# A FiLM layer on one core: other queues for the loads, whole-slab stores, a narrower matmul, program order

## The chip, the cores and the metric

The kernel runs on one core of a Trainium2 chip. The metric is the device time of one execution in microseconds (us). A core has TensorE (PE, matrix products), VectorE (DVE), ScalarE (ACT), GpSimd (POOL) and SyncE (SP). Data move between the main memory and the on-chip memory by 16 DMA engines; in this kernel SP and ACT issue the transfers, and each of the two has a queue of its own on these engines.

## The reference

```python
batch, seq, dim = 32, 512, 256
cond_dim = 64

def reference(x, conditioning, gamma_proj, beta_proj):
    gamma = conditioning @ gamma_proj
    beta = conditioning @ beta_proj
    return (x * (1 + gamma[:, None, :]) + beta[:, None, :]).astype(np.float32)
```

All arrays are float32. x and the output have 32 x 512 x 256 elements, 16.8 MB each. The two projections are small: 32x64 by 64x256.

## The kernel before

The rows of x (batch and seq together, 256 elements each) are cut into four slabs of eight batch entries, 4 MB each. In a slab, partition p holds 32 successive rows, 32 KB, that lie one after the other in the main memory. All four slabs have their own tile (`xs`), so no load ever waits for a buffer. Sixteen partitions belong to one batch entry.

The loads: ACT issues the three small ones, conditioning (`cond_s`, 8 KB), gamma_proj and beta_proj (the two halves of `gbproj`, 64 KB each; lines 48 to 51). SP issues x (line 59): slab 0 in two parts of 8 and 24 rows per partition, the other slabs whole.

The scales: each partition needs the gamma and beta row of its batch entry. An identity of 32x32 is made on GpSimd and each of its columns repeated 16 times on VectorE (`rident`, line 67). One matmul of the conditioning against it gives the transposed conditioning with each column repeated, 64x512 (line 72); VectorE copies it out of PSUM (line 74). For each slab a matmul with 128 of these columns and `gbproj` gives gamma and beta for all 128 partitions, 128x512 in PSUM (`gb_p`, line 79). ACT copies them to `gb_s`, adding one to gamma (lines 82 and 85), because GpSimd works from there; VectorE reads PSUM itself.

The main loop goes over the slabs, and in each over two groups of 16 rows. VectorE takes the first 11 rows of a group and GpSimd the other 5. Each does a multiplication and an addition in place: lines 100 and 103 on VectorE, 102 and 104 on GpSimd. Then ACT issues the store of the group: 16 rows of 128 partitions, 2 MB, in runs of 16 KB (line 105).

A scheduler of the language sets the order of each engine's instructions and places the waits. On VectorE it keeps the order of the program. On GpSimd it puts both multiplications of a slab ahead of both additions. DMA completions are counted on eight semaphores that are used in turn, so the ninth DMA of the program and later ones can wait for the DMA that used the same one before: the last load of x waits in this way for gamma's load.

Of the kernel before, what the change touches and what calls it, by code (L numbers as in the profile page):

```python
# [2 lines left out]

# [5 lines left out]


@with_exitstack
def kernel(
    ctx: ExitStack,
    tc: tile.TileContext,
    x: bass.AP,
    conditioning: bass.AP,
    gamma_proj: bass.AP,
    beta_proj: bass.AP,
    out: bass.AP,  # L20
):
    nc = tc.nc
    f32 = mybir.dt.float32
    ALU = mybir.AluOpType

    batch, seq, dim = x.shape
    cond_dim = conditioning.shape[1]
    P = 128
    SLABS = 4
    BS = batch // SLABS  # L30
    REP = P // BS
    ROWS = BS * seq // P
    assert SLABS * BS == batch and REP * BS == P and ROWS * REP == seq

    x_v = x.flatten_outer_dims().rearrange("(s p r) d -> s p r d", s=SLABS, p=P)
    o_v = out.flatten_outer_dims().rearrange("(s p r) d -> s p r d", s=SLABS, p=P)

    LOADS = {0: [8, 24]}
    GROUP = 16
    ON_DVE = 11  # L40

    consts = ctx.enter_context(tc.tile_pool(name="consts", bufs=1))
    xpool = ctx.enter_context(tc.tile_pool(name="xpool", bufs=1))
    psum = ctx.enter_context(tc.tile_pool(name="psum", bufs=1, space=bass.MemoryType.PSUM))


    cond_s = consts.tile([batch, cond_dim], f32)
    nc.scalar.dma_start(out=cond_s, in_=conditioning)  # L48
    gbproj = consts.tile([cond_dim, 2 * dim], f32)
    nc.scalar.dma_start(out=gbproj[:, :dim], in_=gamma_proj)  # L50
    nc.scalar.dma_start(out=gbproj[:, dim:], in_=beta_proj)

    slabs = []
    for s in range(SLABS):
        xs = xpool.tile([P, ROWS, dim], f32, name=f"xs{s}")
        slabs.append(xs)
        r = 0
        for n in LOADS.get(s, [ROWS]):
            nc.sync.dma_start(out=xs[:, r : r + n, :], in_=x_v[s, :, r : r + n, :])
            r += n  # L60
        assert r == ROWS


    ident = consts.tile([batch, batch], f32)
    make_identity(nc, ident)
    rident = consts.tile([batch, batch * REP], f32)
    nc.vector.tensor_copy(  # L67
        out=rident.rearrange("p (b g) -> p b g", g=REP),
        in_=ident.to_broadcast([batch, batch, REP]),
    )  # L70
    cond_T_p = psum.tile([cond_dim, batch * REP], f32)
    nc.tensor.matmul(cond_T_p, lhsT=cond_s, rhs=rident, start=True, stop=True)  # L72
    cond_T = consts.tile([cond_dim, batch * REP], f32)
    nc.vector.tensor_copy(out=cond_T, in_=cond_T_p)  # L74

    gb_p, gb_s = [], []
    for s in range(SLABS):
        p_t = psum.tile([P, 2 * dim], f32, name=f"gb_p{s}")
        nc.tensor.matmul(p_t, lhsT=cond_T[:, s * P : (s + 1) * P], rhs=gbproj,  # L79
                         start=True, stop=True)  # L80
        s_t = consts.tile([P, 2 * dim], f32, name=f"gb_s{s}")
        nc.scalar.activation(out=s_t[:, :dim], in_=p_t[:, :dim],  # L82
                             func=mybir.ActivationFunctionType.Identity,
                             bias=1.0, scale=1.0)
        nc.scalar.copy(out=s_t[:, dim:], in_=p_t[:, dim:])  # L85
        gb_p.append(p_t)
        gb_s.append(s_t)

    def rows(t, n):
        return bass.AP(tensor=t.tensor, offset=t.offset, ap=[t.ap[0], [0, n], t.ap[1]])  # L90

    for s in range(SLABS):
        xs = slabs[s]
        g_p, b_p = gb_p[s][:, :dim], gb_p[s][:, dim:]
        g_s, b_s = gb_s[s][:, :dim], gb_s[s][:, dim:]
        for r0 in range(0, ROWS, GROUP):
            v = xs[:, r0 : r0 + ON_DVE, :]
            w = xs[:, r0 + ON_DVE : r0 + GROUP, :]
            nv, nw = ON_DVE, GROUP - ON_DVE
            nc.vector.scalar_tensor_tensor(out=v, in0=rows(g_p, nv), scalar=1.0, in1=v,  # L100
                                           op0=ALU.add, op1=ALU.mult)
            nc.gpsimd.tensor_tensor(out=w, in0=w, in1=rows(g_s, nw), op=ALU.mult)  # L102
            nc.vector.tensor_add(out=v, in0=v, in1=rows(b_p, nv))  # L103
            nc.gpsimd.tensor_tensor(out=w, in0=w, in1=rows(b_s, nw), op=ALU.add)  # L104
            nc.scalar.dma_start(out=o_v[s, :, r0 : r0 + GROUP, :],
                                in_=xs[:, r0 : r0 + GROUP, :])


# [1 line left out]
_INS = ['x', 'conditioning', 'gamma_proj', 'beta_proj']  # L110
_OUTS = [((32, 512, 256), 'float32')]


# [23 lines left out]
```

## Time and profile before

| what | value |
|---|---|
| three runs | 84.4, 85.82, 86.3 us; median 85.82 |
| profiled execution | 84.35 us |
| its span, first to last instruction | 82.6 us |
| VectorE busy | 49.9 us (60%) |
| GpSimd busy | 46.2 us (56%) |
| TensorE busy | 9.1 us (11%) |
| DMA | 33.69 MB, mean 408 GB/s over the span |
| first operation on x | 17.3 us (GpSimd), 17.5 us (VectorE) |
| first and last store issued | 25.9 and 66.7 us |
| stores, issue to landing | 15.1 to 22.6 us |

The page gives the busy time of each engine, then rows of 40 digits, each digit the busy tenths of a slice of 2.06 us, then the DMA queues (q1 is SP's, q10 is ACT's), the chain of work that ended last, the groups of instructions with their mean duration, and the DMA issues with their time from issue to landing. The same tables can be asked for a stretch of the span only.

### The profile page before, as it was taken

What the parts mean: (1) busy time and instruction counts of PE and PEld (TensorE: products, weight loads), DVE (VectorE), ACT (ScalarE), POOL (GpSimd) and SP (SyncE); (2) the same over time, 40 slices, a digit from 0 to 9 for tenths busy, and PEclk for the clock granted to TensorE, in tenths of its full rate; (3) what the DMA queues carried; (4) which work ended last, traced back from release to release, by engine and by line L of the source; (5) the groups of instructions that cost most, each with busy time, mean ns of one, the idle gap of its engine ahead of it and who ended that gap; (6) DMA issues with size and microseconds to landing.
All of it is one profiled execution on the core that took longest, in us unless ns stands there. A gap on an engine that the chain in (4) does not pass through costs nothing.

```text
span 82.6 us, 156 instructions
## 1 busy us (share of the span) xinstructions
PE 9.1 (11%) x10; PEld 2.8 (3%) x10; DVE 49.9 (60%) x18; ACT 3.9 (5%) x9; POOL 46.2 (56%) x22
## 2 busy tenths in 40 slices
PE   0080000899600000000000000000000000000000
PEld 0100000443000000000000000000000000000000
DVE  2011000059999999999999999999999920000000
ACT  0600000034400000000000000000000000000000
POOL 2000000069999999999999999999995000000000
DMA  3899999969969989998889979899999999999992
GB/s 56 337 508 397 389 397 524 460 302 508 508 270 492 508 381 381 413 476 381 381 381 556 460 302 460 381 468 421 429 452 389 468 421 421 460 389 452 437 421 87
DMA packets 2080, 33.69 MB, mean 408 GB/s; under 512 B 288, under 2 KB 416, under 8 KB 416
## 3 DMA queue, kind: packets, MB, share of 16 engines
q1 hardware_dynamic: 720, 16.78, 48.6%
q10 hardware_dynamic: 1360, 16.92, 48.0%
HBM read 16.92 MB, written 16.78 MB: 408 GB/s over the span
## 4 chain that ended last, share of the span: by engine, by line
DVE 49%; DMA 16%; issue 11%; PE 2%; ACTq 1%; ACT 1%
DVE xs L100 30%; DVE xs L103 19%; DMA gbproj<-in_beta_proj_dram 16%; PE gb_p L79 2%; ACTq L50 1%; ACTq L48 0%; ACT gb_s L82 0%; ACT gb_s L85 0%
## 5 line engine op out<-in xcount | busy, mean ns | idle before, releaser
L102 POOL TENSOR_TENSOR xs<-xs,gb_s 128x1280 f32<-128x1280 f32 x8 | 23.0, 2895 | 16.2 <-ACT gb_s L82 16.2
L100 DVE SCALAR_TENSOR_TENSOR xs<-gb_p,xs 128x2816 f32<-128x2816 f32 x8 | 24.7, 3083 | 10.9 <-ACT gb_s L85 10.9
L103 DVE TENSOR_TENSOR xs<-xs,gb_p 128x2816 f32<-128x2816 f32 x8 | 24.7, 3086 | 0.3
L104 POOL TENSOR_TENSOR xs<-xs,gb_s 128x1280 f32<-128x1280 f32 x8 | 23.0, 2893 | 0.0
L79 PE MATMUL gb_p<-gbproj,cond_T 64*128 64x512 f32 x8 | 7.2, 1074 | 8.9 <-DMA gbproj<-in_beta_proj_dram 8.9
L74 DVE COPY cond_T<-cond_T_p 64x512 f32<-64x512 f32 x1 | 0.7, 683 | 4.3 <-PE cond_T_p L72 4.3
L79 PEld LDWEIGHTS gb_p<-gbproj,cond_T 64*128 64x128 f32 x8 | 2.5, 328 | 13.7 <-issue 13.7
L72 PE MATMUL cond_T_p<-rident,cond_s 32*64 32x512 f32 x2 | 1.9, 1065 | 3.9 <-DMA cond_s<-in_conditioning_dram 3.9
L82 ACT ACTIVATE gb_s<-gb_p 128x256 f32<-128x256 f32 x4 | 1.5, 383 | 16.4 <-PE gb_p L79 16.4
L85 ACT COPY gb_s<-gb_p 128x256 f32<-128x256 f32 x4 | 1.5, 367 | 0.0
L82 ACT ACT_TABLE_LOAD x1 | 1.3, 1283 | 2.4 <-issue 2.4
L67 DVE COPY rident<-ident 32x512 f32<-32x512 f32 x1 | 0.4, 416 | 1.2 <-POOL ident masks.py:199 1.2
L72 PEld LDWEIGHTS cond_T_p<-rident,cond_s 32*64 32x64 f32 x2 | 0.3, 202 | 3.9 <-issue 3.9
masks.py:197 POOL MEMSET ident<- 32x32 f32 x1 | 0.1, 114 | 0.3 <-POOLq L121 0.3
masks.py:199 POOL TENSOR_SCALAR_AFFINE_SELECT ident<-ident 32x32 f32<-32x32 f32 x1 | 0.2, 202 | 0.1
L121 POOL MEMSET const-float32-0.0<- 128x1 f32 x1 | 0.1, 103 | 0.2 <-issue 0.2
L121 POOL MEMSET const-bfloat16-1.0<- 128x1 bf16 x1 | 0.1, 106 | 0.0
L121 POOL MEMSET const-uint8-127<- 128x1 uint8 x1 | 0.1, 106 | 0.0
L121 POOL MEMSET const-float32-1.0<- 128x1 f32 x1 | 0.1, 103 | 0.0
## 6 DMA issues: line engine op xcount, KB each, us to landing
out_dram<-xs ACTq DMA_DIRECT2D x8, 2048.0 KB, 18.2
xs<-in_x_dram SPq DMA_DIRECT2D x3, 4096.0 KB, 32.9
xs<-in_x_dram SPq DMA_DIRECT2D x1, 3072.0 KB, 12.2
xs<-in_x_dram SPq DMA_DIRECT2D x1, 1024.0 KB, 4.6
gbproj<-in_gamma_proj_dram ACTq DMA_DIRECT2D x1, 64.0 KB, 9.1
gbproj<-in_beta_proj_dram ACTq DMA_DIRECT2D x1, 64.0 KB, 12.9
cond_s<-in_conditioning_dram ACTq DMA_DIRECT2D x1, 8.0 KB, 3.0
```

Source lines behind the costliest of these rows:

```text
L50: nc.scalar.dma_start(out=gbproj[:, :dim], in_=gamma_proj)
L67: nc.vector.tensor_copy(out=rident.rearrange("p (b g) -> p b g", g=REP), in_=ident.to_broadcast([batch, batch, REP]),)
L72: nc.tensor.matmul(cond_T_p, lhsT=cond_s, rhs=rident, start=True, stop=True)
L74: nc.vector.tensor_copy(out=cond_T, in_=cond_T_p)
L79: nc.tensor.matmul(p_t, lhsT=cond_T[:, s * P : (s + 1) * P], rhs=gbproj, start=True, stop=True)
L82: nc.scalar.activation(out=s_t[:, :dim], in_=p_t[:, :dim], func=mybir.ActivationFunctionType.Identity, bias=1.0, scale=1.0)
L85: nc.scalar.copy(out=s_t[:, dim:], in_=p_t[:, dim:])
L100: nc.vector.scalar_tensor_tensor(out=v, in0=rows(g_p, nv), scalar=1.0, in1=v, op0=ALU.add, op1=ALU.mult)
L102: nc.gpsimd.tensor_tensor(out=w, in0=w, in1=rows(g_s, nw), op=ALU.mult)
L103: nc.vector.tensor_add(out=v, in0=v, in1=rows(b_p, nv))
L104: nc.gpsimd.tensor_tensor(out=w, in0=w, in1=rows(b_s, nw), op=ALU.add)
L121: nc = _bacc.Bacc("TRN2", target_bir_lowering=False, num_devices=1)
```

## The change

It has four parts. The first 8 rows per partition of x are loaded by ACT; the three small loads go to SP, ahead of the rest of x. The matmul that transposes the conditioning uses the plain 32x32 identity and gives 64x32; the 16-fold repetition is made afterwards, for each slab, in VectorE's copy out of PSUM (four copies of 64x128 for one of 64x512). Each slab is stored at once, 4 MB in runs of 32 KB, after both of its groups of 16 rows. The main loop stands in a block that keeps the order of the program, so that GpSimd multiplies and adds one group before it takes the next. The sizes of slabs and groups, and the 11 to 5 split of rows, are as before. The last load of x now waits for the first load of x instead of gamma's.

```diff
-    LOADS = {0: [8, 24]}
-    GROUP = 16
-    ON_DVE = 11
+    SLABS = [(8, [8, 24]), (8, [32]), (8, [32]), (8, [32])]
+    STORES = [[32], [32], [32], [32]]
+    PIECE, ON_DVE = 16, 11
...
+    def load(eng, s, i):
+        sl = slabs[s]
+        r = sum(sl["loads"][:i])
+        n = sl["loads"][i]
+        eng.dma_start(out=sl["xs"][:, r : r + n, :], in_=sl["src"][:, r : r + n, :])
...
-    nc.scalar.dma_start(out=cond_s, in_=conditioning)
-    nc.scalar.dma_start(out=gbproj[:, :dim], in_=gamma_proj)
-    nc.scalar.dma_start(out=gbproj[:, dim:], in_=beta_proj)
...
-        for n in LOADS.get(s, [ROWS]):
-            nc.sync.dma_start(out=xs[:, r : r + n, :], in_=x_v[s, :, r : r + n, :])
...
+    load(nc.scalar, 0, 0)
+    nc.sync.dma_start(out=cond_s, in_=conditioning)
+    nc.sync.dma_start(out=gbproj[:, :dim], in_=gamma_proj)
+    nc.sync.dma_start(out=gbproj[:, dim:], in_=beta_proj)
+    load(nc.sync, 0, 1)
+    load(nc.sync, 1, 0)
+    load(nc.sync, 2, 0)
+    load(nc.sync, 3, 0)
...
-    rident = consts.tile([batch, batch * REP], f32)
-    nc.vector.tensor_copy(
-        out=rident.rearrange("p (b g) -> p b g", g=REP),
-        in_=ident.to_broadcast([batch, batch, REP]),
-    )
-    cond_T_p = psum.tile([cond_dim, batch * REP], f32)
-    nc.tensor.matmul(cond_T_p, lhsT=cond_s, rhs=rident, start=True, stop=True)
-    cond_T = consts.tile([cond_dim, batch * REP], f32)
-    nc.vector.tensor_copy(out=cond_T, in_=cond_T_p)
...
+    cond_T_p = psum.tile([cond_dim, batch], f32)
+    nc.tensor.matmul(cond_T_p, lhsT=cond_s, rhs=ident, start=True, stop=True)
+    for s, sl in enumerate(slabs):
...
+        c_t = consts.tile([cond_dim, P], f32, name=f"cond_T{s}")
+        nc.vector.tensor_copy(
+            out=c_t.rearrange("p (b g) -> p b g", g=rep),
+            in_=cond_T_p[:, b0 : b0 + n].to_broadcast([cond_dim, n, rep]),
+        )
...
+        nc.tensor.matmul(p_t, lhsT=c_t, rhs=gbproj, start=True, stop=True)
...
-            nc.scalar.dma_start(out=o_v[s, :, r0 : r0 + GROUP, :],
-                                in_=xs[:, r0 : r0 + GROUP, :])
+    with tc.manual_schedule():
+        for s, sl in enumerate(slabs):
...
+            for n in STORES[s]:
+                for q0 in range(done, done + n, PIECE):
...
+                nc.scalar.dma_start(out=sl["dst"][:, done : done + n, :],
+                                    in_=xs[:, done : done + n, :])
```

More of the change, by code (lines that the diff above doesn't have):

```diff
@@ L28 @@
     P = 128
[L29 to L36, printed above, removed]
-    LOADS = {0: [8, 24]}
-    GROUP = 16
-    ON_DVE = 11
+    SLABS = [(8, [8, 24]), (8, [32]), (8, [32]), (8, [32])]
+    assert sum(n for n, _ in SLABS) == batch
+    STORES = [[32], [32], [32], [32]]
+    PIECE, ON_DVE = 16, 11
+    x_f = x.flatten_outer_dims()
+    o_f = out.flatten_outer_dims()
     consts = ctx.enter_context(tc.tile_pool(name="consts", bufs=1))
@@ L44 @@
     psum = ctx.enter_context(tc.tile_pool(name="psum", bufs=1, space=bass.MemoryType.PSUM))
+    slabs = []
+    b0 = 0
+    for s, (n, loads) in enumerate(SLABS):
+        assert P % n == 0
+        rows = n * seq // P
+        r0, r1 = b0 * seq, (b0 + n) * seq
+        slabs.append(dict(
+            n=n, b0=b0, rows=rows, loads=loads,
+            src=x_f[r0:r1, :].rearrange("(p r) d -> p r d", p=P),
+            dst=o_f[r0:r1, :].rearrange("(p r) d -> p r d", p=P),
+            xs=xpool.tile([P, rows, dim], f32, name=f"xs{s}"),
+        ))
+        b0 += n
@@ L47 @@
+    def load(eng, s, i):
[3 more added lines that the diff above has]
+        eng.dma_start(out=sl["xs"][:, r : r + n, :], in_=sl["src"][:, r : r + n, :])
     cond_s = consts.tile([batch, cond_dim], f32)
-    nc.scalar.dma_start(out=cond_s, in_=conditioning)
     gbproj = consts.tile([cond_dim, 2 * dim], f32)
-    nc.scalar.dma_start(out=gbproj[:, :dim], in_=gamma_proj)
-    nc.scalar.dma_start(out=gbproj[:, dim:], in_=beta_proj)
[L53 to L57, printed above, removed]
-        for n in LOADS.get(s, [ROWS]):
-            nc.sync.dma_start(out=xs[:, r : r + n, :], in_=x_v[s, :, r : r + n, :])
-            r += n
-        assert r == ROWS
+    load(nc.scalar, 0, 0)
@@ L71 @@
-    cond_T_p = psum.tile([cond_dim, batch * REP], f32)
-    nc.tensor.matmul(cond_T_p, lhsT=cond_s, rhs=rident, start=True, stop=True)
-    cond_T = consts.tile([cond_dim, batch * REP], f32)
-    nc.vector.tensor_copy(out=cond_T, in_=cond_T_p)
-    gb_p, gb_s = [], []
-    for s in range(SLABS):
+    gb_p, gb_s = [], []
+    cond_T_p = psum.tile([cond_dim, batch], f32)
+    nc.tensor.matmul(cond_T_p, lhsT=cond_s, rhs=ident, start=True, stop=True)
+    for s, sl in enumerate(slabs):
+        n, b0 = sl["n"], sl["b0"]
+        rep = P // n
+        c_t = consts.tile([cond_dim, P], f32, name=f"cond_T{s}")
[3 more added lines that the diff above has]
+        )
@@ L78 @@
         p_t = psum.tile([P, 2 * dim], f32, name=f"gb_p{s}")
-        nc.tensor.matmul(p_t, lhsT=cond_T[:, s * P : (s + 1) * P], rhs=gbproj,
-                         start=True, stop=True)
+        nc.tensor.matmul(p_t, lhsT=c_t, rhs=gbproj, start=True, stop=True)
         s_t = consts.tile([P, 2 * dim], f32, name=f"gb_s{s}")
@@ L87, with spread @@
         gb_s.append(s_t)
-    def rows(t, n):
+    def spread(t, n):
         return bass.AP(tensor=t.tensor, offset=t.offset, ap=[t.ap[0], [0, n], t.ap[1]])
[L92 to L104, printed above, removed]
-            nc.scalar.dma_start(out=o_v[s, :, r0 : r0 + GROUP, :],
-                                in_=xs[:, r0 : r0 + GROUP, :])
+    with tc.manual_schedule():
+        for s, sl in enumerate(slabs):
+            xs = sl["xs"]
+            g_p, b_p = gb_p[s][:, :dim], gb_p[s][:, dim:]
+            g_s, b_s = gb_s[s][:, :dim], gb_s[s][:, dim:]
+            done = 0
+            for n in STORES[s]:
+                for q0 in range(done, done + n, PIECE):
+                    nv, nw = ON_DVE, PIECE - ON_DVE
+                    v = xs[:, q0 : q0 + nv, :]
+                    w = xs[:, q0 + nv : q0 + PIECE, :]
+                    nc.vector.scalar_tensor_tensor(out=v, in0=spread(g_p, nv), scalar=1.0, in1=v,
+                                                   op0=ALU.add, op1=ALU.mult)
+                    nc.gpsimd.tensor_tensor(out=w, in0=w, in1=spread(g_s, nw), op=ALU.mult)
+                    nc.vector.tensor_add(out=v, in0=v, in1=spread(b_p, nv))
+                    nc.gpsimd.tensor_tensor(out=w, in0=w, in1=spread(b_s, nw), op=ALU.add)
+                nc.scalar.dma_start(out=sl["dst"][:, done : done + n, :],
+                                    in_=xs[:, done : done + n, :])
+                done += n
+            assert done == sl["rows"]
 _INS = ['x', 'conditioning', 'gamma_proj', 'beta_proj']
```

## The prediction

> **What bounds the kernel now.** I read the page's overview first, then the two DMA queues stretch by stretch, then the chain of waits, then the groups of instructions. The overview with its 40 slices, and the DMA totals:
>
> ```profile
> span 82.6 us, 156 instructions
> ...
> DVE  2011000059999999999999999999999920000000
> ACT  0600000034400000000000000000000000000000
> POOL 2000000069999999999999999999995000000000
> DMA  3899999969969989998889979899999999999992
> ...
> HBM read 16.92 MB, written 16.78 MB: 408 GB/s over the span
> ```
>
> The DMA row is full from slice 2 to slice 39. VectorE works only from slice 9 to slice 32, and nothing but DMA goes on in the last fifth. The bytes, 16.92 + 16.78 = 33.69 MB, start to move at about 1.5 us (the first packets) and the last data packet ends at about 81 us: 33.69 / 79.5 = 0.424 MB per us. The question is whether the engines could move them faster. The queue table, cut to 15 to 20 us (loads alone), then 35 to 40 us (both), then 60 to 65 us (stores alone); columns: packets, MB, share of the 16 engines' time. q1 carries SP's transfers, q10 ACT's:
>
> ```profile
> q1 hardware_dynamic: 68, 2.23, 103.1%
> ```
> ```profile
> q1 hardware_dynamic: 41, 1.34, 62.2%
> q10 hardware_dynamic: 45, 0.74, 34.4%
> ```
> ```profile
> q10 hardware_dynamic: 149, 2.18, 101.8%
> ```
>
> Loads alone: 5 us x 16 engines x 1.031 / 68 = 1.21 us for a packet of 2.23 / 68 = 32.8 KB, or 27 KB per us and engine. Stores: 133 data packets of 16.4 KB make the 2.18 MB (the rest are completion writes), 81.4 us / 133 = 0.61 us each, the same 27 KB per us. So 16 engines give about 0.432 MB per us whichever way the data goes and whether the run is 16 or 32 KB. At 0.424 the kernel is within 2% of it. **DMA bytes set the end**, not the following chain, which is the chain of waits in order of time (start, length, what):
>
> ```profile
> 1.72 12.90 DMA gbproj<-in_beta_proj_dram
> ...
> 17.52 3.10 DVE xs L100
> ...
> 63.49 3.09 DVE xs L103
> ```
>
> It ends at 66.6, when the last multiply-add is done. The last store is issued there and lands 15.1 us later (the shortest landing of the eight stores), at 81.8. Two MB alone would take 2.1 / 0.432 = 4.9 us: the other 10 us are stores queued ahead of it. That backlog is the slack of everything upstream.
>
> The middle fence is the second thing to see. While both queues have work, 41 packets of one go beside 45 of the other: turns are equal in number, not in bytes. A load's packet is a 32 KB run, a store's a 16 KB run, so loads get 1.34 of 2.08 MB, two thirds.
>
> [...] the trace shows 2.18 MB in 5 us, 436. [...]
>
> **The change part by part.** Rows that the sums use (count | busy us, mean ns), and issues (KB, us to landing):
>
> ```profile
> L102 POOL TENSOR_TENSOR xs<-xs,gb_s 128x1280 f32<-128x1280 f32 x8 | 23.0, 2895 | 16.2 <-ACT gb_s L82 16.2
> L100 DVE SCALAR_TENSOR_TENSOR xs<-gb_p,xs 128x2816 f32<-128x2816 f32 x8 | 24.7, 3083 | 10.9 <-ACT gb_s L85 10.9
> L103 DVE TENSOR_TENSOR xs<-xs,gb_p 128x2816 f32<-128x2816 f32 x8 | 24.7, 3086 | 0.3
> ...
> xs<-in_x_dram SPq DMA_DIRECT2D x1, 3072.0 KB, 12.2
> ...
> gbproj<-in_beta_proj_dram ACTq DMA_DIRECT2D x1, 64.0 KB, 12.9
> ```
>
> *Order of the loads.* Before, gamma and beta on ACT's queue take turns with x packets of 8, 24 and 32 KB on SP's; beta's last packet lands at 1.72 + 12.9 = 14.6. After, the three small loads stand ahead of x on SP's queue and share turns only with the first 1 MB of x, whose packets are 8 KB, 0.31 us each at 27 KB per us. Per engine these are 8 turns, 2.5 us. ACT's issues took 0.40, 0.51 and 0.61 us; at that price SP issues beta by 1.7 and the rest of x from 2.3. SP's x issues slide 1.5 us, covered by the first MB, which starts on ACT at the same 0.74 and keeps the engines busy from 1.5 to 4. If that cover failed, it would cost up to 1.5 us of idle DMA. The fifth x load waits for the landing of an earlier DMA in both kernels; that is gamma at 10.3 before and the first x load, near 5, after. Nothing stands behind it on SP, and x packets are queued ahead, so this is worth 0. Beta should land between 4 and 6.
>
> *Narrow matmul.* Out go the spread of the identity (416 ns), two 512-wide passes (1065 ns each) and one 683 ns copy; in come two 32-wide passes and four copies of 64x128. [...] The trace has no 32-wide pass: above 0, below 1.07 us; I take 0.1. The first projection then starts with beta near 5, takes 2.06 (two passes before), and the two ACT copies 0.65: ready by 8 against 17.3. Both bounds leave it ahead of the x it meets, since each slab's first piece spans rows 0 to 16 and so needs the second x load. That had landed at about 1.4 + 12.2 = 13.6 and has the same 4.3 MB ahead of it. So VectorE starts at 13.7, not 17.5: 3.8 us gained upstream, 0 at the end.
>
> *Program order and whole-slab stores.* A slab is 2 x (3.08 + 3.09) = 12.35 us on VectorE and 4 x 2.89 = 11.6 on GpSimd. In program order GpSimd's add directly follows its multiply; VectorE does this already at about 0.03 us. Between 0 and 0.2 us each, and even 0.8 a slab only fills the 0.75 by which GpSimd is ahead. Slab 0 is done at 13.7 + 12.35 = 26.1; before, the first store was issued at 25.9. So the earlier start is spent on the larger store. ACT waits for the slab with nothing but later stores behind it; four issues of 0.34 us are gone, worth 0 off the path.
>
> *32 KB store runs.* Before, the first store packets ran from 29, when about 11.7 MB of x had moved; the same holds after. The remaining 5.1 MB of x are 5.1 / (16 x 0.0328) = 9.7 turns per engine. Before, a turn with its store was 1.21 + 0.61 = 1.82 us: 17.7 us, so 46.7; the last x load in fact landed at 10.3 + 39.2 = 49.5, 2.8 us later [...]. After, a turn is 2.42 us: 29 + 23.5 + 2.8 = 55.3. **A new stall**: VectorE is through slabs 1 and 2 at 26.1 + 24.7 = 50.8 and waits 4.5 us for slab 3. Slab 3 is done at 55.3 + 12.35 = 67.7, and its 4.2 MB are issued then.
>
> Is the DMA still busy then? At 29, 11.8 MB have moved. What remains before the last store is 5.1 of x and 12.58 of stores, 17.7 MB; at the mean 0.427 of the mixed stretch, 41.4 us: 70.4. Issue and start take 0.34 + about 0.8 (the first x load: issued 0.74, first packet 1.5), so the last store is ready at 68.9, with **1.5 us of cover**. It then needs 4.19 / 0.427 = 9.8 us: 80.2, plus the 1.6 by which before's own sum (29 + 21.9 / 0.427 = 80.2) falls short of its 81.8. End 81.8, change 0. The sum: +0 (loads) +0 (matmul) +0 (stores) on the profiled 84.35, which is the span of 82.6 and 1.75 around it. The median of the three runs, 85.82, is 1.47 higher; the forecast in terms of that median is 85.7, no change.
>
> **The rivals.**
>
> *Slower: the cover is eaten.* One mechanism: x gets less than half while stores are queued, so slab 3 lands late and the engines run dry before the last, undivided 4 MB. At a share of 43%, a turn is 1.21 / 0.43 = 2.81 us: slab 3 lands at 29 + 27.3 + 2.8 = 59.1, is done at 71.5, moves from 72.6, ends at 72.6 + 9.8 + 1.6 = 84.0: +2.2 us, 88.0 in the median's terms. It decides from a landing at 56.8, and passes 2% (1.7 us) at 58.5. For it: the last x load was already 2.8 us later than its turns, and the last store now has no smaller one after it. Against: turns are even in the trace.
>
> *Faster: the DMA gets its last few per cent.* If all bytes moved at 0.436: 33.69 / 0.436 = 77.3, from 1.5 on, with 0.8 for landing, ends at 79.6, so -2.2 us, 83.6. For it: turns become equal, small packets go in one burst. Against: 16 and 32 KB runs moved equally fast, and that window is the best one.
>
> *It doesn't do what it says*: if stores still go in 16 KB packets, x keeps two thirds, slab 3 lands near 49.5, VectorE ends at 13.7 + 4 x 12.35 = 63.1, and backlog again sets the end: 85.7. Only the trace would tell it.
>
> **How the numbers follow.** Forecast 0.50, unsplit packets' rival 0.10, slower 0.27, faster 0.13. Of the slower case 0.23 lies over 2%, of the faster 0.11; 2% is about what a measurement of this kernel can tell from no change. Faster 0.11, same 0.66, slower 0.23. Range: 84.0, near the faster case (0.13 mostly below or at it), to 87.8, just short of the slower case, which leaves about 2 in 10 outside; it also holds the runs of before, 84.4 to 86.3.
>
> **What would show it.** Right: beta landed by 6; VectorE starting near 13.7; a stall of about 4.5 us on slab 3's load; equal bytes on both queues from 30 to 50 us; DMA full to the end. Wrong: empty DMA slices around 70 us, a last x load after 57, a mean rate well above 0.427, or a gap in the DMA before 5 us.

## The result, and the profile after

The changed kernel is slower, by little: the ratio to the kernel before is 1.0128, with a 95% interval of 1.0093 to 1.0163, some 1.1 us. The median of its six runs is 85.66 us (85.23 to 85.84), that of the kernel before 85.2 us. The medians lie closer than the ratio because some executions of the kernel before take about 1.5 us longer than the rest, and the ratio leaves them out. The forecast was no change, at 85.7, within 84.0 to 87.8. That 85.66 lies so near 85.7 is luck: 85.7 stood for no change from a first median of 85.82, and what the ratio compares with is 85.66 / 1.0128 = 84.6. The forecast of no change was wrong, and what follows looks for 1.1 us.

The profiled execution took 85.23 us, with a span of 83.4. The page of the changed kernel, overview, DMA totals and queues (q1 is SP's, q10 ACT's: packets, MB, share of the 16 DMA engines):

```profile
span 83.4 us, 152 instructions
...
DVE  0400002999999999999999993006999992000000
ACT  4100334100000000000000000000000000000000
POOL 2000002999999999999999960006999990000000
DMA  2899989979989979999999999999999999999980
...
q10 hardware_dynamic: 720, 17.83, 50.0%
q1 hardware_dynamic: 784, 15.87, 45.7%
HBM read 16.92 MB, written 16.78 MB: 404 GB/s over the span
```

VectorE now starts in slice 7 instead of 9 and stands still for most of slices 25 to 28, as forecast. The DMA row is full up to the end: the DMA engines were not left without stores. The two queue shares add up to 95.7% of 83.4 us, 79.8 us of packets per engine. Before it was 48.6% and 48.0% of 82.6 us, 79.8 too. **The DMA engines do the same work and take 0.8 us longer over it.** Nor were the long packets slower in themselves: 32 KB packets of the stores took 1.213 us each, twice the 0.611 of 16 KB.

The chain of waits of the changed kernel, in order of time:

```profile
1.75 0.58 SPq L70
2.34 0.04 issue
2.38 11.56 DMA xs<-in_x_dram
...
14.06 3.10 DVE xs L114
...
50.90 6.07 another core or an unknown queue
...
57.09 3.10 DVE xs L114
...
66.34 3.09 DVE xs L117
```

The 6.07 us are the wait for slab 3; its load was issued at 6.5 and took 50.4 us, to 56.9. The last store is issued at 69.5 and lands 12.9 us later.

Where did the DMA fall back? Stretches of 2 us of the kernel before, then of the changed one. The last column is GB/s, the one ahead of it the busy share of the DMA engines:

```profile
4.00:6.00 2.00, 1.85 (x2) 0.18 (x2) 0.11 (x1) 0.00 (x0) 0.00 (x0) 1.00 1.30 553
...
28.00:30.00 2.00, 0.00 (x0) 0.00 (x0) 2.00 (x2) 0.00 (x0) 2.00 (x2) 1.00 0.90 336
```
```profile
4.00:6.00 2.00, 0.00 (x0) 0.00 (x0) 0.18 (x1) 0.00 (x0) 0.00 (x0) 1.00 1.26 426
...
28.00:30.00 2.00, 0.00 (x0) 0.00 (x0) 1.97 (x2) 0.00 (x0) 1.92 (x2) 1.00 0.86 262
```

These rates put a packet's bytes at its start, so single figures are coarse, but two places stand out: 4 to 6 us, where the small loads pass, and 28 to 30 us, where the first store joins the loads. A finer measure comes from the packet records: the bytes moved up to a moment, divided by 0.432 MB per us (the rate worked out in the prediction), and taken from the time since the first packet. That is the **lag**: the time that the missing bytes would take at that rate, as a mean over the engines. The first packet starts 1.75 us after the start of the span in both kernels.

And there is the end. The last store ends with 16 completion packets of 4 bytes, as many as there are DMA engines; I read them as one from each engine (the records don't name it). The queue in 81.0 to 81.4 us, kernel before:

```profile
q10 hardware_dynamic: 16, 0.00, 2.2%
```

All 16 come in these 0.4 us. The changed kernel in 81.0 to 81.4, and in 81.4 to 82.2:

```profile
q10 hardware_dynamic: 6, 0.00, 0.8%
```
```profile
q10 hardware_dynamic: 10, 0.00, 0.7%
```

Six have come, and ten come later. By the records the first and the last completion lie 0.32 us apart before and 0.88 after. I call this the **spread**. The kernel's end goes with the last of the 16: it comes at 81.39 us in a span of 82.6 before, and at 82.03 in one of 83.4 after.

### The profile page after: what moved, and what is told of

It reads as the page before. It is cut to its first block, busy times and chain, and to the rows that moved or that the text cites. A ratio compares the mean times of both kernels' runs of the same rounds, so it can differ in the third digit from the quotient of the medians.

```text
span 83.4 us, 152 instructions
## 1 busy us (share of the span) xinstructions
PE 7.6 (9%) x10; PEld 2.8 (3%) x10; DVE 49.8 (60%) x20; ACT 3.9 (5%) x9; POOL 46.6 (56%) x22
## 4 chain that ended last, share of the span: by engine, by line
DVE 54%; DMA 14%; another core or an unknown queue 7%; issue 5%; SPq 2%; DVEq 0%
DVE xs L114 29%; DVE xs L117 25%; DMA xs<-in_x_dram 14%; SPq L70 1%; SPq L69 1%; SPq L68 0%; DVEq L114 0%
## 5 line engine op out<-in xcount | busy, mean ns | idle before, releaser
L86 DVE COPY cond_T<-cond_T_p 64x128 f32<-64x128 f32 x4 | 0.9, 274 | 3.3 <-PE cond_T_p L81 3.3
```

Source lines behind the costliest of these rows:

```text
L86: nc.vector.tensor_copy(out=c_t.rearrange("p (b g) -> p b g", g=rep), in_=cond_T_p[:, b0 : b0 + n].to_broadcast([cond_dim, n, rep]),)
```

## The experiments

The runs fall into four sets. Each set has its own runs of the kernel before, and a ratio is to these.

### The two edits alone, and each undone

Only the stores changed in the kernel before:

```diff
-            nc.scalar.dma_start(out=o_v[s, :, r0 : r0 + GROUP, :],
-                                in_=xs[:, r0 : r0 + GROUP, :])
+        nc.scalar.dma_start(out=o_v[s], in_=xs)
```

> Kernel before with one part of the change: each slab stored at once, 32 KB runs. Two theories on where the changed kernel's 1.1 us go. S (stores): when the first whole-slab store meets the loads, load packets are slowed for longer (28 to 30 us moved 262 GB/s against 336), and the 16 engines finish further apart. L (loads): the new order of the loads leaves a hole after the first megabyte (4 to 6 us moved 426 GB/s against 553). S expects most of the loss here: +0.5 to +1.1 us, ratio 1.006 to 1.013. L expects 1.000.

Measured: 1.0004 (0.9992 to 1.0015). Whole-slab stores by themselves cost nothing. Theory S, as put, falls.

Only the load order changed in the kernel before:

```diff
-    nc.scalar.dma_start(out=cond_s, in_=conditioning)
...
+            eng = nc.scalar if (s, r) == (0, 0) else nc.sync
+            eng.dma_start(out=xs[:, r : r + n, :], in_=x_v[s, :, r : r + n, :])
+            if (s, r) == (0, 0):
+                nc.sync.dma_start(out=cond_s, in_=conditioning)
+                nc.sync.dma_start(out=gbproj[:, :dim], in_=gamma_proj)
+                nc.sync.dma_start(out=gbproj[:, dim:], in_=beta_proj)
```

> Kernel before with one part of the change: first x load on ACT, small loads and the rest of x on SP. L expects the loss here, +0.5 to +1.1 us, ratio 1.006 to 1.013, and VectorE starting at 14. S expects at most +0.2 us, ratio 1.000 to 1.003. That an earlier start of the work is worth nothing in itself is common to both.

Measured: 1.0051 (1.0028 to 1.0075), 0.4 us. The order of the loads costs something.

The changed kernel with half-slab stores:

```diff
-    STORES = [[32], [32], [32], [32]]
+    STORES = [[16, 16], [16, 16], [16, 16], [16, 16]]
```

> Changed kernel with the stores in halves again (16 rows, 16 KB runs): all but the whole-slab stores. S expects the time of the kernel before, ratio 0.998 to 1.003, the last x load landing near 50 and no stall before slab 3. L expects what the load order alone gives. If the narrow matmul and the program order cost anything, this run differs from the load order alone; I expect no difference (0.2 us at most).

Measured: 1.0053 (1.0036 to 1.0069).

The changed kernel with the old order of the loads:

```diff
-    load(nc.scalar, 0, 0)
-    nc.sync.dma_start(out=cond_s, in_=conditioning)
-    nc.sync.dma_start(out=gbproj[:, :dim], in_=gamma_proj)
-    nc.sync.dma_start(out=gbproj[:, dim:], in_=beta_proj)
+    nc.scalar.dma_start(out=cond_s, in_=conditioning)
+    nc.scalar.dma_start(out=gbproj[:, :dim], in_=gamma_proj)
+    nc.scalar.dma_start(out=gbproj[:, dim:], in_=beta_proj)
+    load(nc.sync, 0, 0)
```

> Changed kernel with the load order of before: small loads on ACT, all x on SP; whole-slab stores, narrow matmul and program order stay. S expects the time of the changed kernel, ratio 1.008 to 1.013; L expects the time of before, 1.000 to 1.003. VectorE starts near 17.5 and, as the first store goes out near 30, the last x load should land some 3 us earlier than in the changed kernel, 54.

Measured: 1.0005 (0.9994 to 1.0015). The last two runs hold the narrow matmul and the program order as well, and equal their counterparts without them (1.0053 beside 1.0051, 1.0005 beside 1.0004): **those two parts are worth nothing**, as forecast. But the parts do not add: load order 0.5%, stores 0, both 1.3%. So the changed kernel ran again, beside the next three:

> The changed kernel once more, beside the runs below. The parts gave: whole-slab stores 1.000, load order 1.005. If they simply add, this gives 1.005 to 1.006 here, and the 1.013 of the first comparison held the accident of its runs. If early start and whole-slab stores harm each other, it gives 1.010 or more again, with 28 to 30 us at a low rate (262 GB/s before) and the last x load landing after 56.

Measured: 1.0098 (1.0064 to 1.0133), median 85.57 us. Some 0.5% are the load order's, and the rest goes when either edit is undone.

### The hole behind the small loads

What does the load order do at 4 to 6 us? By the packet records, the 8 KB packets of the first x load run on ACT's queue until about 3 us after the first packet. The 128 packets of gamma and beta (0.046 us each) start only then, and ahead of the 3 MB that stand behind them on SP's queue. So they took no turns with the first megabyte; they came after it. Of the first 16 of the 24 KB packets behind them, 15 took 1.28 to 1.45 us where the form usually takes 0.912. In the kernel before the same packets follow the 8 KB ones directly, with 0.912 us from the first, and the small ones are spread among them, 3.9 to 11.1 us after the first packet. There too gamma and beta took no turns with the first megabyte. ACT's queue in the kernel before, 2 to 5 and 5 to 10 us of the span:

```profile
q10 hardware_dynamic: 48, 0.01, 1.5%
```
```profile
q10 hardware_dynamic: 80, 0.07, 3.9%
```

The first 48 packets are the conditioning's alone (32 with data, 16 completions). Gamma's load was issued at 1.2 us, but its packets start at 5.6, when the first megabyte is through. Why they wait for it is not shown. Three runs move the small loads about.

```diff
+    load(nc.sync, 0, 1)
     nc.sync.dma_start(out=cond_s, in_=conditioning)
     nc.sync.dma_start(out=gbproj[:, :dim], in_=gamma_proj)
     nc.sync.dma_start(out=gbproj[:, dim:], in_=beta_proj)
-    load(nc.sync, 0, 1)
```

> Changed kernel, but on SP the 3 MB of x's second load go ahead of the three small loads. Hole theory: whenever an engine has nothing but the small packets and what stands behind them in the same queue, it moves next to nothing for a moment[...]. Then the hole moves from 4-6 us to about 11-13 us and the time stays that of the changed kernel (within 0.2 us). Order theory: the loss comes from splitting x's first loads over two queues; then it stays in 4-6 us. A third: what costs is that small packets come before any large one on SP; then it is gone and the time is that of before.

Measured: 1.0012 (0.9987 to 1.0038). The hole did move: the lag is 0.88 us at 6 us after the first packet and 1.48 at 20. Yet the time is that of the kernel before, which my hole theory did not expect. Two things differ: the lag did not grow at the first store (1.47 at 24, 1.42 at 40), and the spread stayed at 0.65. So small loads ahead of a large one are not enough to lose time; here they stand behind the first large load of their queue. Why the same hole costs nothing 6 us later is not shown.

```diff
-    nc.sync.dma_start(out=cond_s, in_=conditioning)
-    nc.sync.dma_start(out=gbproj[:, :dim], in_=gamma_proj)
-    nc.sync.dma_start(out=gbproj[:, dim:], in_=beta_proj)
+    nc.scalar.dma_start(out=cond_s, in_=conditioning)
+    nc.scalar.dma_start(out=gbproj[:, :dim], in_=gamma_proj)
+    nc.scalar.dma_start(out=gbproj[:, dim:], in_=beta_proj)
```

> Changed kernel, but the three small loads stay on ACT, behind the first x load; SP carries the rest of x from the start. x's first loads are on two queues as in the changed kernel, but no large transfer stands behind a small one. Hole theory: no hole in 4 to 6 us, engines finishing within 0.6 us of each other, ratio 0.998 to 1.002. Order theory: 1.005 or more. VectorE starts near 15 to 18.

Measured: 1.1131 (1.1087 to 1.1176), 94.43 us. The hole is gone (lag 0.92 at 6), but something far larger came. From the chain of waits of this run:

```profile
2.20 26.34 DMA gbproj<-in_beta_proj_dram
...
31.43 3.10 DVE xs L114
```

Now SP's large packets run from the start, and the packets on ACT's queue take turns with them, about one for one: 32 of 8 KB beside 29 of 24 KB in 8 to 10 us, then 64 of the small loads (1 KB or less) beside 63 of 32 KB in 15 to 20. Beta lands at 28.5, VectorE starts at 31.4, the first store goes out at 43.8, and by then all loads are done. From there every store runs alone and lands in 11.1 us, and the DMA waits for VectorE: four slabs take 31.4 to 80.6, and 80.6 + 11.1 = 91.7. This kernel is bound by compute.

```diff
     load(nc.scalar, 0, 0)
+    load(nc.scalar, 0, 1)
...
-    load(nc.sync, 0, 1)
```

> Changed kernel, but ACT issues both loads of slab 0 (1 and 3 MB); SP issues the small loads and slabs 1 to 3. The small loads still come before large ones on SP's queue, but ACT's queue has large packets beside them until about 15 us. Hole theory (an engine left with small packets alone loses time on the next large one): no hole in 4 to 6 us, lower spread at the end, ratio 0.998 to 1.004. If small before large in one queue is enough by itself: a loss as in the changed kernel, 1.005 to 1.013. Slab 0 shares its turns with slab 1, so VectorE starts later than 14, near 17.

Measured: 1.0013 (1.0002 to 1.0024). The small loads still stand ahead of large ones on SP's queue, but ACT's 3 MB run beside them. The stretch from 4 to 6 us:

```profile
4.00:6.00 2.00, 0.00 (x0) 0.00 (x0) 0.11 (x1) 0.00 (x0) 0.00 (x0) 1.00 1.26 536
```

536 against 426 GB/s; lag 0.74 at 6 us, spread 0.40. So the loss goes when the DMA engines have large packets to move beside the small ones.

### The first store

The changed kernel with the last slab alone stored in halves:

```diff
-    STORES = [[32], [32], [32], [32]]
+    STORES = [[32], [32], [32], [16, 16]]
```

> Changed kernel with the last slab stored in two halves, the first of them some 6 us earlier. If the backlog of stores ever ran out on one of the engines before the last store (my prediction's slower case), this gives back 0.4 us or more. If the DMA engines were never without work, as the trace of the changed kernel shows, it changes nothing: within 0.2 us of the changed kernel beside it.

Measured: 1.0103 (1.0053 to 1.0153), like the changed kernel beside it. The end of the backlog is not the cause. Slab 0 alone stored in halves:

```diff
-    STORES = [[32], [32], [32], [32]]
+    STORES = [[16, 16], [32], [32], [32]]
```

> Changed kernel with slab 0 alone stored in two halves, the first of them near 20 us. If the second part of the loss (some 0.4 us beyond the load order's 0.5%) comes from 4 MB of 32 KB store runs meeting the loads at once at 26.5, it goes: ratio near 1.005 and 28 to 30 us near 430 GB/s. If it comes from the later whole-slab stores or from the late last load, it stays: 1.010.

Measured: 1.0047 (1.0029 to 1.0065). The second part of the loss is gone, and only the load order's is left. The first half goes out at 20.2 us, where the whole slab went at 26.5. The changed kernel with its first store some 4 us later:

```diff
+    pad = consts.tile([P, 15, dim], f32)
+    nc.gpsimd.memset(pad, 0.0)
+
     with tc.manual_schedule():
+        nc.vector.tensor_add(out=pad, in0=pad, in1=slabs[0]["xs"][:, 8:23, :])
```

> Changed kernel with one added VectorE addition of about 4 us into a tile of its own ahead of slab 0 (it reads 15 rows of slab 0, its result goes nowhere), so that the first store is issued near 30.5 and not 26.5. Everything else stays, the hole at 4 to 6 us too. If the early start of whole-slab stores makes the second part of the loss: ratio near 1.005, faster than the changed kernel although VectorE works 4 us more. If the loss is all in the loads: that of the changed kernel, 1.010.

Measured: 1.0112 (1.0085 to 1.0139). It stays, and the dip moves along with the store, issued at 30.6 now: the lag is 1.00 at 24 us and 1.74 at 40. So a later moment does not help, and the dip belongs to the first store, whenever it comes. Whether an earlier moment would help is not tested: the half store above is both smaller and earlier.

The two edits together in the kernel before, without the other two (both edits as above):

> Kernel before with the new load order and whole-slab stores, but the wide matmul and the scheduler's order. Alone the load order gave 1.005 and the stores 1.000. If these two harm each other, this gives the changed kernel's 1.010 to 1.013, with 28 to 30 us near 262 GB/s. If the second part of the loss needs the narrow matmul or the program order, it gives 1.005.

Measured: 1.0075 (1.0049 to 1.0100), median 85.5 us. The interval takes in both cases, 1.005 and 1.010. In this set the kernel before ran longer than elsewhere (median 84.95 us, 40 runs, against 84.54 to 84.6 in the other sets), so a median from it can't be held against those of other sets either. The dip at the first store is there as in the changed kernel (lag 1.15 at 24 us, 2.04 at 40). That the two edits are enough without the other two is likely, and not shown.

The changed kernel with slab 0 stored by two DMAs of 16 KB runs, written one behind the other at the end of the slab:

```diff
-                nc.scalar.dma_start(out=sl["dst"][:, done : done + n, :],
-                                    in_=xs[:, done : done + n, :])
+                h = n // 2 if s == 0 else n
+                for c in range(done, done + n, h):
+                    nc.scalar.dma_start(out=sl["dst"][:, c : c + h, :],
+                                        in_=xs[:, c : c + h, :])
```

> Changed kernel with slab 0 alone stored by two DMAs of 16 KB runs, both issued when the whole slab is done, at 26.5. If the length of the first store's runs (32 KB) makes the second part: ratio near 1.005, as with the halves issued one by one (1.0047). If it is the late start, or that 4 MB are queued at once: 1.010 still.

Measured: 1.0057 (1.0022 to 1.0092), median 85.42 us. But the edit did not do what was meant. The two stores in the timeline of this run (start, length with the gap between them):

```profile
20.64 6.47 ACTq L121 DMA_DIRECT2D out_dram<-xs  x2
```

ACT issued the first half at 20.6 us, as soon as its rows were done, and the second at 26.8. That is the run with the halves once more (20.2 and 26.3 there), and it agrees with it: 1.0057 beside 1.0047, and a small dip (lag 1.08 at 20 us and 1.42 at 40, there 1.11 and 1.49). Its spread is the widest of all, 1.50 us. So length, amount and moment of the first store were never tested apart: in the runs with the hole, halves go out at 20.1 to 22.5 us, whole slabs at 26.1 to 30.6. Nor does this set tell its own two runs apart, 85.42 us with the half and 85.5 with the whole slab; that a half is better rests on the halved and the later first store further up, which belong to one set (84.97 against 85.49), and on the half-slab stores (1.0053).

### The cover, measured

```diff
+    pad = consts.tile([P, ON_DVE, dim], f32)
+    nc.gpsimd.memset(pad, 0.0)
...
+                    if s == 3 and q0 == PIECE:
+                        nc.vector.tensor_add(out=pad, in0=pad, in1=pad)
```

> Changed kernel with one added VectorE addition of 3.1 us, on a tile of its own, in the middle of slab 3, so that the last store is issued near 72.6 and not 69.5. In the changed kernel that store lands 12.9 us after its issue; where nothing is queued ahead, a 4 MB store took 11.1. So 1.8 us of cover are left there, and 3.1 us of delay should cost 1.3 us over the changed kernel (ratio 1.022 to 1.028 to the kernel before). If the cover were used up already, it would cost all 3.1 (1.046).

Measured: 1.0524 (1.0503 to 1.0546), 89.02 us, more than either case. The reason is that the added operation took 5.5 us, not 3.1 (see the end): the last store went out at 74.9, 5.4 us later than in the changed kernel, and cost 89.02 - 85.57 = 3.4 us. So 2.0 us were covered, where 12.9 - 11.1 = 1.8 were expected. With the DMA out of work before it, the last store's completions lie 0.15 us apart, as they do in the kernel that compute bounds.

### Both remedies together

The two loads of slab 0 on ACT, and slab 0 stored in halves:

> The two remedies together: both loads of slab 0 on ACT (1.0013 alone), and slab 0 alone stored in halves. No hole at 4 to 6 us, and a smaller dip at the first store. If both parts of the loss are understood, 0.998 to 1.001, the kernel before or a little less.

Measured: 84.55 us (22 runs), 0.9951 (0.9928 to 0.9973) beside the kernel before of that set, which ran longer. 84.55 is also the median that the kernel before has in the other sets, so I don't call it faster than before; in its own set it is 0.95 us better than the kernel with both edits (85.5). Its completion packets, 80.75 to 81.25 us:

```profile
q10 hardware_dynamic: 16, 0.00, 1.8%
```

### All runs side by side

Lag in us at 6, 24 and 40 us after the first packet, and spread of the last store's completions, from the packet records of one profile each (the two kernels in which the DMA ran out of work are left out):

| kernel | ratio | median us | lag 6 / 24 / 40 | spread |
|---|---|---|---|---|
| before | 1 | 84.54 to 84.6 (three sets) | 0.68 / 1.00 / 1.42 | 0.32 |
| whole-slab stores alone | 1.0004 | 84.66 | 0.77 / 1.00 / 1.48 | 0.58 |
| after, old load order | 1.0005 | 84.55 | 0.82 / 1.39 / 1.34 | 0.58 |
| small loads after 3 MB | 1.0012 | 84.72 | 0.88 / 1.47 / 1.42 | 0.65 |
| slab 0 on ACT | 1.0013 | 84.66 | 0.74 / 1.03 / 1.63 | 0.40 |
| slab 0 on ACT, its store halved | 0.9951 | 84.55 | 0.76 / 1.02 / 1.37 | 0.34 |
| load order alone | 1.0051 | 85.04 | 1.05 / 1.20 / 1.65 | 0.87 |
| after, half-slab stores | 1.0053 | 84.98 | 1.28 / 1.55 / 1.56 | 1.00 |
| after, slab 0's store halved | 1.0047 | 84.97 | 1.14 / 1.49 / 1.49 | 1.06 |
| after, slab 0 in two at once | 1.0057 | 85.42 | 1.12 / 1.31 / 1.42 | 1.50 |
| load order and whole stores | 1.0075 | 85.5 | 1.18 / 1.15 / 2.04 | 1.11 |
| after, first store later | 1.0112 | 85.49 | 1.05 / 1.00 / 1.74 | 1.07 |
| after, last store halved | 1.0103 | 85.58 | 1.29 / 1.25 / 1.99 | 1.15 |
| after | 1.0128, 1.0098 | 85.66, 85.57 | 1.24 / 1.20 / 1.92 | 0.88 |

The table falls into three blocks. Without the hole at the start, the spread is at most 0.65 and the time that of before. With it, the spread is 0.87 or more and the time 0.4 us longer than that of before in the same set. With it and a whole-slab first store, the lag grows by 0.7 to 0.9 us at that store (0.63 or less in the other rows, counted from 20 us), and the time is about a microsecond longer (0.6 with the two edits in the kernel before). The mean lag alone doesn't order the rows: at 40 us it is 1.34 to 1.63 in the first block and 1.42 to 1.65 in the second. The blocks were made after the runs, from one profile each.

## Why the prediction was wrong

**What held.** DMA bytes set the end in both kernels. Turns went by packets: with 32 KB on both queues, loads and stores shared evenly, as 30 to 35 us of the changed kernel shows (32 packets of each):

```profile
q1 hardware_dynamic: 32, 1.05, 52.0%
q10 hardware_dynamic: 32, 1.05, 48.5%
```

From this came the last x load at 55.3 (measured 56.9), the new stall of 4.5 us (6.2) and the last store behind 67.7 (issued at 69.5). VectorE started at 14.06 (forecast 13.7). Narrow matmul and program order cost nothing. The rival in which the engines run dry before the last store did not come about: the cover forecast as 1.5 us is about 1.8 to 2.0, and halving the last store brings nothing. By the prediction's sum a last load at 56.8 would have used the cover up; it came at 56.97, so the cover was put too small. The earlier start was worth nothing, as said.

**The step that failed** is the one on the order of the loads: "covered by the first MB", worth 0. It rested on the small loads sharing turns with that megabyte. Gamma and beta did not; they passed after it, with the 3 MB of x behind them in the same queue, so the DMA engines lost half a microsecond each in the mean: the lag rises from 0.73 at 3 us to 1.24 at 6. This order by itself costs 0.4 us (1.0051), and its loss is gone with the old order (1.0005), with the small loads behind the 3 MB (1.0012), and with large packets beside them (1.0013). That much is shown.

How the hole comes to cost 0.4 us is read from the packet records, not tested. In the kernel before the small loads cost time too (0.67 at 3 us, 1.00 at 20), so the mean loses only 0.2; with the load order alone it is 1.02 at 20, and loses nothing. What I left out is the distance between the engines, read from the completions of a transfer. My sum treated the 16 as one pipe, at the mean rate of the kernel before, in which such a loss can't appear. An engine that falls behind at the start seems to keep its distance: the completions of slab 0's 3 MB lie 0.73 us apart, those of the last three stores 0.88; with the load order alone 0.79 and 0.87; before, 0.31 and 0.32. (In between, while loads and stores run together, they lie up to 1.97 apart in the changed kernel; the records don't name the engine, so none can be followed.) One run does not fit: with the small loads behind the 3 MB that slab's completions lie 0.84 apart, the last store's 0.65, and no time is lost. The last data of the changed kernel moved 80.27 us after the first packet, against 79.64: 0.63 of the 0.8 us of the span, of which 0.39 is the mean's lag (1.84 against 1.45 at 70 us) and the rest spread. The trace of before could have told part of this: it has gamma and beta beside packets of 24 and 32 KB, but not, as the prediction read it, beside those of 8 KB. It never has them alone. I put the price of a failed cover at up to 1.5 us and a gap before 5 us among the signs of being wrong, so the size was in sight; the chance was not.

**A second step was incomplete**: that the first store packets join at 29 and "the same holds after" (they join at 29.8 before and 30.3 after). Alone that is right, but behind the hole the dip at the first whole-slab store is larger, and costs another 0.5 us. That this takes the new load order and an undivided first store is shown in the changed kernel. Whether the store's length, amount or moment counts is not, nor why engines that are apart should suffer more from it: the records show load packets of up to 2.15 us there instead of 1.21 (up to 1.66 in the kernel before), but no cause.

Beta was forecast to land by 4 to 6 and came at 6.9, since its packets ran only after the first megabyte; VectorE's wait for x hid it. A small misreading did no harm: the second x load of the kernel before was issued at 1.2 and landed at 13.4, not 1.4 and 13.6.

## What to carry to other kernels

In this kernel, which DMA bytes bound, the end went with the last completion of the 16 DMA engines (spread 0.88 us after, 0.32 before), not with their mean alone: look at how far apart the completion packets of one transfer lie. Tiny loads ahead of the first large load of a queue cost 0.4 us here when the other queue had run dry (1.0051), and nothing with large packets on the other queue (1.0013), or behind the first large load (1.0012). But small packets that took turns with large ones, about one for one, and stood behind 8 KB packets with turns of their own, landed 26 us after their issue. VectorE's start at 14.06 us instead of 17.52 was worth nothing, as the store backlog covered it, and the cover can be read off: time to landing of the last store, less that of such a store alone (12.9 - 11.1 = 1.8 us here).

## What the runs showed that I had not expected

The added addition with both inputs in SBUF (the on-chip memory that the tiles of x lie in) took 5.5 us beside GpSimd, where additions of the same size with one input in PSUM take 3.09, and GpSimd's next operation took 5.6 instead of 2.9. The timeline of that run:

```profile
62.88 2.88 POOL L121 TENSOR_TENSOR xs<-xs,gb_s 128x1280 f32<-128x1280 f32 x1
63.17 5.53 DVE L117 TENSOR_TENSOR pad<-pad 128x2816 f32<-128x2816 f32 x1
65.83 5.62 POOL L123 TENSOR_TENSOR xs<-xs,gb_s 128x1280 f32<-128x1280 f32 x1
68.62 3.08 DVE L119 SCALAR_TENSOR_TENSOR xs<-gb_p,xs 128x2816 f32<-128x2816 f32 x1
```

The addition ends at 68.70, 2.94 us after GpSimd's operation (65.76), and GpSimd's next ends at 71.45, 2.75 us after the addition. The numbers fit two operations that each waited for the other engine's to end and then took about their own length: GpSimd's take 2.89, and the addition in the run with the later first store took 4.16 us for 3840 elements, with GpSimd idle all that time, which scaled to 2816 elements gives an estimate of 3.05. This is read from one timeline; the cause was not tested. In this kernel VectorE takes gamma and beta from PSUM, one input of each operation, and such operations keep to 3.08 and 3.09 us beside GpSimd's 2.89.
